# A DoRA forward kernel on Trainium2: joint runs of DRAM rows for blocks 3 and 4 and for block 6 with half of block 7, and one row stored apart

## The chip, the cores and the metric

The kernel runs on one core of one Trainium2 chip. That core has a matrix engine (TensorE, called PE in the profile, with its weight loads as PEld), a vector engine (DVE), a scalar engine (ACT), a general engine (POOL) and a synchronising engine (SP), an on-chip memory of 128 partitions (SBUF), a smaller one for matrix results (PSUM), and 16 DMA engines that move data between SBUF and DRAM. Times are device microseconds of one execution. Before the change the median of 7 runs is 163.18 us, the lowest 162.53 and the highest 163.72.

## The reference

```
W_adapted    = W + scale * (lora_A @ lora_B)
W_norm       = sqrt(sum(W_adapted ** 2, axis=0) + 1e-8)
W_final      = W_adapted / W_norm * m
y            = x.reshape(-1, 256) @ W_final
```

x has 16 x 2048 = 32768 rows of 256 float32 numbers, so a row is 1 KB and x is 32 MB; y has the same size. W is 256 x 256, the rank of lora_A and lora_B is 16. Every row of y depends on the same row of x alone, so rows may be handled in any order, as long as a result goes back to the place that its row came from.

## The kernel before

**Blocks, chunks, buffers.** The 32768 rows form 8 blocks of 4096. A block fills one buffer in SBUF, with 32 rows in each of the 128 partitions, and there are 5 buffers (`XBUFS`); block b uses buffer b mod 5. A block is 8 chunks (`CH`), a chunk 4 rows in each partition (`J`). Chunks are numbered 0 to 63 through all blocks. Results are written over the x rows that they were made from, in the same buffer, and stored from there.

**Rows in DRAM.** Which rows of x a partition gets is set by `units` (L101, L102). A unit is a stretch of consecutive rows in DRAM that is dealt out to the 128 partitions in equal consecutive runs. Before, each of the blocks 0 to 6 is one unit, so a partition's run is 32 rows, 32 KB, and the runs of neighbouring partitions begin 32 KB apart. Block 7 is two units of 16 rows each. `transfer` (L137) finds the unit of a transfer's first chunk and moves the wanted part of each partition's run, for loads and stores alike.

**Loads.** `loads` (L111 to L114) lists first chunk, count of chunks and rows in one DMA. Blocks 1, 2 and 3 come in one DMA of 4 MB each, block 4 as 24 rows and twice 4 rows, blocks 5 to 7 in halves. SP issues all of them in order; blocks 5, 6 and 7, and the last 8 rows of block 4, wait for the stores that free their buffers or that are to go first.

**Stores.** `stores` (L116 to L122) lists first chunk, count, rows in one DMA, and the chunk after which ACT issues it. The entries before `FIRST` are blocks 0 to 2. Then come, of block 3, four DMAs of 4 rows after chunk 27 and one after chunk 28; the remaining 12 rows of block 3 and all of block 4 as two DMAs after chunk 44; block 5 after chunk 47, block 6 after chunk 55, and the halves of block 7 after chunks 59 and 63. ACT drains its own writes before it issues (L282).

**The work on a chunk.** POOL rounds x to bfloat16 in pairs of chunks (L208), PE turns it (L321), DVE copies the turned block out of PSUM (L248), PE multiplies with the final weights (L335), and ACT copies the product over x in SBUF (L276). A short prologue makes the weights.

**The end.** The stores from `FIRST` on have semaphores of their own, and SP waits for each of them in turn and clears it (L360). `pieces` says how far a semaphore counts: 16 for every DMA of an entry.

Of the kernel before, what the change touches and what calls it, by code (L numbers as in the profile page):

```python
# [11 lines left out]
def kernel(  # L12
# [11 lines left out]
    P = 128  # L24
    FP32 = mybir.dt.float32
# [6 lines left out]
    N, IN = x_flat.shape  # L32
# [3 lines left out]
    J = 4  # L36
    DJ = 32
    BLK = DJ * P
    NBLK = N // BLK
# [3 lines left out]
    XBUFS = 5  # L43
    CH = DJ // J
    NCH = NBLK * CH
# [16 lines left out]
    def sb(name, shape, dtype):  # L62
        return ctx.enter_context(nc.sbuf_tensor(name, shape, dtype))
# [1 line left out]
    def ps(name, shape, dtype):  # L65
        return ctx.enter_context(nc.psum_tensor(name, shape, dtype))

    x_bufs = [sb(f"x_sb{k}", [P, DJ, IN], FP32) for k in range(XBUFS)]
    xb_bufs = [sb(f"xb{k}", [P, 2 * J, IN], BF16) for k in range(NXB)]
    xt_bufs = [sb(f"xt{k}", [P, F8, KC], BF16) for k in range(NXT)]  # L70
    w_nat = sb("w_nat", [P, KC, OUT], FP32)
# [26 lines left out]

    units = [(b * CH, CH) for b in range(NBLK - 1)]  # L101
    units += [(NCH - CH, CH // 2), (NCH - CH // 2, CH // 2)]  # L102

# [2 lines left out]
    F = NBLK - XBUFS  # L108
    G = F * CH
# [6 lines left out]
    stores = [(b * CH, CH, CH * J, 19 + b) for b in range(F - 1)]  # L116
    stores += [(G - CH, 3, 3 * J, G), (G - 5, 5, 5 * J, G)]
    FIRST = len(stores)
    stores += [(G, 4, J, G + 3), (G + 4, 1, J, G + 4)]
    stores += [(G + 5, CH - 5, (CH - 5) * J, 44), (G + CH, CH, CH * J, 44)]  # L120
    stores += [(b * CH, CH, CH * J, (b + 1) * CH - 1) for b in range(F + 2, NBLK - 1)]
    stores += [(g0, cnt, cnt * J, g0 + cnt - 1) for g0, cnt in units[-2:]]  # L122

    def pieces(entry):

        return 16 * (entry[1] * J // entry[2])


    late = [nc.alloc_semaphore(f"store{n}") for n in range(FIRST, len(stores))]
    sems = {f"store{FIRST + k}": s for k, s in enumerate(late)}  # L130

    def sem(name):
        if name not in sems:
            sems[name] = tc.alloc_semaphore(name)
        return sems[name]

    def transfer(engine, name, entry, dram, store):  # L137
        g0, cnt, rows = entry[:3]
        b, c = divmod(g0, CH)
        (u0, ucnt), = [u for u in units if u[0] <= g0 < u[0] + u[1]]  # L140
        unit = dram[u0 * J * P : (u0 + ucnt) * J * P].rearrange("(p j) k -> p j k", p=P)
        for r in range(0, cnt * J, rows):
            here = x_bufs[b % XBUFS][:, c * J + r : c * J + r + rows, :]
            there = unit[:, (g0 - u0) * J + r : (g0 - u0) * J + r + rows, :]
            src, dst = (here, there) if store else (there, here)
            engine.dma_start(out=dst, in_=src).then_inc(sem(name), 16)

    def load_x(n):
        transfer(nc.sync, f"load{n}", loads[n], x_flat, False)

    def store_y(n):
        transfer(nc.scalar, f"store{n}", stores[n], out_flat, True)

    def wait_load(engine, g):
        engine.wait_ge(sem(f"load{load_of[g]}"), pieces(loads[load_of[g]]))

    def wait_store(engine, n):
        engine.wait_ge(sem(f"store{n}"), pieces(stores[n]))
# [3 lines left out]
        out=w_nat[:], in_=W.rearrange("(p t) o -> p t o", t=KC)  # L162
    ).then_inc(sem("load_w"), 16)
    nc.scalar.dma_start(
        out=a_nat[:], in_=lora_A.rearrange("(p t) r -> p t r", t=KC)
# [3 lines left out]
    for n in range(len(loads)):  # L169
# [14 lines left out]
        out=identity[:],  # L184
        in_=zeros[:],
# [7 lines left out]
    for p in range(1, NPR):  # L193
        b, c = divmod(p, PRB)
# [9 lines left out]
        if p == REST:  # L204
            wait_store(nc.gpsimd, FIRST - 2)
        if p >= NXB:
            nc.gpsimd.wait_ge(sem("turned"), p - NXB + 1)
        nc.gpsimd.tensor_copy(  # L208
            out=xb_bufs[p % NXB][:],
            in_=x_bufs[b % XBUFS][:, 2 * c * J : 2 * (c + 1) * J, :],  # L210
# [15 lines left out]
        out=wa[:], in0=ab_ps, scalar=float(scale), in1=w_nat[:], op0=ALU.mult, op1=ALU.add  # L226
# [19 lines left out]
    for p in range(NPR):  # L246
        nc.vector.wait_ge(sem("turned"), p + 1)
        nc.vector.tensor_copy(  # L248
            out=xt_bufs[p % NXT][:].rearrange("p r t -> p (r t)").bitcast(FP32),
            in_=xt_ps[p % 2][:],  # L250
# [4 lines left out]
    for engine, idle in ((nc.gpsimd, 8), (nc.vector, 24)):  # L255
# [13 lines left out]
        out=norm[:], in_=n2_ps, func=AF.Sqrt, bias=eps_col[:]  # L269
    ).then_inc(sem("act"), 1)  # L270
    drains = 0
    for g in range(NCH):
        b, c = divmod(g, CH)
# [3 lines left out]
            out=x_bufs[b % XBUFS][:, c * J : (c + 1) * J, :], in_=y_ps[g % 2][:]  # L277
# [80 lines left out]
    for k, s in enumerate(late):  # L358
        nc.sync.wait_ge(s, pieces(stores[FIRST + k]))
        nc.sync.sem_clear(s)  # L360
# [35 lines left out]
```

## Time and profile before

| what | value |
|---|---|
| median of 7 runs | 163.18 us |
| the profiled execution | 163.25 us, span 161.9 us |
| PE busy | 94.8 us (59%) |
| ACT, POOL, DVE busy | 66.1, 60.7, 44.9 us |
| moved over DMA | 67.43 MB in 4645 packets, mean 416 GB/s |
| HBM read, written | 33.85 MB, 33.55 MB |
| last store issued by ACT | 131.46 us |

The span runs from the first to the last instruction that the profiler recorded; the execution's own time is 1.35 us more. The 40 slices of the page are each about 4 us long, a digit is a busy share in tenths. A DMA packet is one contiguous piece that one DMA engine moves. The trace also holds each packet's start, time and size, though not its engine, and the moment at which each DMA engine reports its share of a transfer as landed.

### The profile page before, as it was taken

To read this page: it belongs to the slowest core of one execution; us is meant where nothing else is said; L and a number is where in the kernel's file an instruction comes from. 1 tells how busy PE (TensorE), PEld (TensorE's weight loads), DVE (VectorE), ACT (ScalarE), POOL (GpSimd) and SP (SyncE) were. 2 spreads that over 40 slices of the span, in tenths; PEclk is the share of its full clock that TensorE was granted. 3 is DMA by queue.
4 is the path that set the end of the run, shared out by engine and by line. 5 is a ranking of instruction groups with operands and counts; after the bars stand their busy time and mean duration, and the time that the engine had idled before them with its cause. 6 is when DMAs were issued, how large, how long until landed. Compare 5 with 4: busy or idle time off the path is not lost. (4 is left out here: it accounts for less than half of the span.)

```text
span 161.9 us, 2027 instructions
## 1 busy us (share of the span) xinstructions
PE 94.8 (59%) x786; PEld 83.8 (52%) x786; DVE 44.9 (28%) x44; ACT 66.1 (41%) x68; POOL 60.7 (37%) x38
## 2 busy tenths in 40 slices
PE   0594986999999600000699999989988910000000
PEld 0282866999989400000689999979977900000000
DVE  0567233354444300000124535344533300000000
ACT  3320582767777610000047686677684640000000
POOL 1045319677672000001947675864839000000000
PEclk9998799999999985555579999999999995555555
DMA  4999999999999999999999999999999999999994
GB/s 158 431 443 465 405 478 413 413 469 413 421 388 364 494 405 397 429 413 460 405 430 423 437 424 427 443 420 415 444 492 400 413 480 407 405 486 405 397 441 206
DMA packets 4645, 67.43 MB, mean 416 GB/s; under 512 B 657, under 2 KB 674, under 8 KB 1698
## 3 DMA queue, kind: packets, MB, share of 16 engines
q1 hardware_dynamic: 2304, 33.82, 49.5%
q10 hardware_dynamic: 2338, 33.59, 48.6%
q14 instruction: 3, 0.02, 0.0%
HBM read 33.85 MB, written 33.55 MB: 416 GB/s over the span
## 5 line engine op out<-in xcount | busy, mean ns | idle before, releaser
L276 ACT COPY x_sb<-y_ps 128x1024 f32<-128x1024 f32 x64 | 62.2, 1015 | 58.7 <-PE y_ps L335 55.6
L208 POOL CAST xb<-x_sb 128x2048 bf16<-128x2048 f32 x31 | 58.2, 1893 | 64.0 <-DMA x_sb<-in_x_dram 29.3
L335 PE MATMUL y_ps<-w_final,xt 128*128 128x256 bf16 x512 | 64.7, 281 | 3.9 <-PEq L311 3.8
L248 DVE COPY xt<-xt_ps 128x1024 f32<-128x1024 f32 x32 | 39.1, 1224 | 75.0 <-PE xt_ps L321 74.9
L335 PEld LDWEIGHTS y_ps<-w_final,xt 128*128 128x128 bf16 x512 | 51.4, 101 | 11.7 <-issue 4.9
L321 PE MATMUL xt_ps<-identity,xb 128*128 128x128 f32 x264 | 35.9, 282 | 25.8 <-PEq L311 25.8
L321 PEld LDWEIGHTS xt_ps<-identity,xb 128*128 128x128 f32 x264 | 31.5, 147 | 27.2 <-issue 26.7
L264 ACT CAST xb<-x_sb 128x2048 bf16<-128x2048 f32 x1 | 1.9, 1899 | 2.7 <-DMA x_sb<-in_x_dram 2.7
L292 PE MATMUL y_ps<-identity,a_nat 128*16 128x128 f32 x2 | 0.6, 394 | 4.0 <-DMA a_nat<-in_lora_A_dram 4.0
L305 PE MATMUL y_ps<-sq,ones 128*128 128x256 f32 x4 | 2.1, 674 | 0.7 <-DVE sq L229 0.7
L262 ACT ACT_TABLE_LOAD x1 | 1.3, 1283 | 2.4 <-issue 2.4
L292 PEld LDWEIGHTS y_ps<-identity,a_nat 128*16 128x16 f32 x2 | 0.1, 90 | 4.0 <-issue 4.0
L238 DVE RECIPROCAL rnorm<-norm 128x256 f32<-128x256 f32 x1 | 1.8, 1753 | 1.5 <-ACT norm L268 1.5
L305 PEld LDWEIGHTS y_ps<-sq,ones 128*128 128x128 f32 x4 | 1.2, 323 | 1.6 <-DVE sq L229 1.5
L214 POOL MEMSET xb<- 128x2048 bf16 x1 | 1.8, 1804 | 0.0
L220 DVE CAST b_bf<-b_nat 16x256 bf16<-16x256 f32 x1 | 0.3, 281 | 3.8 <-DMA b_nat<-in_lora_B_dram 3.8
L296 PE MATMUL y_ps<-b_bf,aT 16*128 16x256 bf16 x2 | 0.6, 402 | 1.0 <-DVE aT L222 1.0
L268 ACT ACTIVATE norm<-y_ps,eps_col 128x256 f32<-128x256 f32 x1 | 0.5, 474 | 1.5 <-PE y_ps L305 1.5
L301 PE MATMUL y_ps<-m_row,ones 1*128 1x256 f32 x2 | 1.1, 630 | 0.0
L296 PEld LDWEIGHTS y_ps<-b_bf,aT 16*128 16x128 bf16 x2 | 0.1, 104 | 1.5 <-DVE aT L222 1.5
L225 DVE SCALAR_TENSOR_TENSOR wa<-y_ps,w_nat 128x512 f32<-128x512 f32 x1 | 0.7, 692 | 0.8 <-PE y_ps L296 0.8
L235 DVE TENSOR_TENSOR wam<-wa,m_all 128x256 f32<-128x256 f32 x2 | 0.8, 421 | 0.0
(14 smaller groups left out, 4.1 us busy)
## 6 DMA issues: line engine op xcount, KB each, us to landing
out_dram<-x_sb ACTq DMA_DIRECT2D x5, 4096.0 KB, 27.7
x_sb<-in_x_dram SPq DMA_DIRECT2D x7, 2048.0 KB, 29.4
x_sb<-in_x_dram SPq DMA_DIRECT2D x3, 4096.0 KB, 30.1
out_dram<-x_sb ACTq DMA_DIRECT2D x2, 2048.0 KB, 30.6
x_sb<-in_x_dram SPq DMA_DIRECT2D x1, 3072.0 KB, 47.7
out_dram<-x_sb ACTq DMA_DIRECT2D x2, 1536.0 KB, 20.7
out_dram<-x_sb ACTq DMA_DIRECT2D x1, 2560.0 KB, 32.9
out_dram<-x_sb ACTq DMA_DIRECT2D x5, 512.0 KB, 40.7
```

The source lines that it names most:

```text
L208: nc.gpsimd.tensor_copy(out=xb_bufs[p % NXB][:], in_=x_bufs[b % XBUFS][:, 2 * c * J : 2 * (c + 1) * J, :],).then_inc(sem("rounded"), 1)
L214: nc.gpsimd.memset(xb_bufs[NPR % NXB][:], 0.0).then_inc(sem("rounded"), 1)
L235: i = nc.vector.tensor_mul(out=wam[:, t], in0=wa[:, t], in1=m_all[:])
L238: nc.vector.reciprocal(out=rnorm[:], in_=norm[:]).then_inc(dv, 1)
L248: nc.vector.tensor_copy(out=xt_bufs[p % NXT][:].rearrange("p r t -> p (r t)").bitcast(FP32), in_=xt_ps[p % 2][:],).then_inc(sem("copied"), 1)
L262: nc.scalar.activation(out=warm[:], in_=eps_col[:], func=AF.Sqrt)
L264: nc.scalar.copy(out=xb_bufs[0][:], in_=x_bufs[0][:, 0 : 2 * J, :]).then_inc(sem("early"), 1)
L276: nc.scalar.copy(out=x_bufs[b % XBUFS][:, c * J : (c + 1) * J, :], in_=y_ps[g % 2][:]).then_inc(sem("room"), 1)
L301: nc.tensor.matmul(mb_ps, ones[0:1, :], m_row[:], start=True, stop=True).then_inc(pe, 1)
L305: i = nc.tensor.matmul(n2_ps, ones[:], sq[:, t, :], start=(t == 0), stop=(t == KC - 1))
L321: i = nc.tensor.transpose(xt_ps[p % 2][:, j * P : (j + 1) * P], xb_bufs[p % NXB][:, j, :].bitcast(FP32), identity[:],)
L335: i = nc.tensor.matmul(y_ps[h][:, j, :], xt_bufs[p % NXT][:, r : r + P, t], w_final[:, t, :], start=(t == 0 and (j % (J // 2)) == 0), stop ...
```

## The change

The units change. Blocks 3 and 4 become one unit of 64 rows in each partition, block 6 and the first half of block 7 one of 48 rows. Blocks 0, 1, 2 and 5 and the second half of block 7 stay as they were. So that a transfer can reach over two buffers, the five buffers become slices of one tensor `x_sb`.

The stores follow. The last 12 rows of block 3 and the 32 rows of block 4 become one entry of 44 rows, after chunk 44 as before. Block 6 and half of block 7 become one of 48 rows after chunk 59; block 6 was stored after chunk 55 before.

The entry of 44 rows, `stores[ODD]`, is issued as three DMAs: 43 rows of all 128 partitions, then the last row of the partitions 0 to 124, then the last row of the other three. They are the row "by 125 and 3 partitions on five DMA engines" of the change's description. `pieces` counts 48 for the entry. The late stores are six entries instead of eight.

The loads keep their list; those of blocks 3, 4, 6 and 7 read at other places in DRAM, by the new units.

```
-    x_bufs = [sb(f"x_sb{k}", [P, DJ, IN], FP32) for k in range(XBUFS)]
+    x_sb = sb("x_sb", [P, XBUFS * DJ, IN], FP32)
+    x_bufs = [x_sb[:, k * DJ : (k + 1) * DJ, :] for k in range(XBUFS)]
...
-    units = [(b * CH, CH) for b in range(NBLK - 1)]
-    units += [(NCH - CH, CH // 2), (NCH - CH // 2, CH // 2)]
+    units = [(b * CH, CH) for b in range(3)]
+    units += [(3 * CH, 2 * CH), (5 * CH, CH), (6 * CH, CH + CH // 2)]
+    units += [(NCH - CH // 2, CH // 2)]
...
     FIRST = len(stores)
+    ODD = FIRST + 2
     stores += [(G, 4, J, G + 3), (G + 4, 1, J, G + 4)]
-    stores += [(G + 5, CH - 5, (CH - 5) * J, 44), (G + CH, CH, CH * J, 44)]
-    stores += [(b * CH, CH, CH * J, (b + 1) * CH - 1) for b in range(F + 2, NBLK - 1)]
-    stores += [(g0, cnt, cnt * J, g0 + cnt - 1) for g0, cnt in units[-2:]]
+    stores += [(G + 5, 2 * CH - 5, (2 * CH - 5) * J, 44)]
+    stores += [(g0, cnt, cnt * J, g0 + cnt - 1) for g0, cnt in units[-3:]]
 
     def pieces(entry):
+        if entry is stores[ODD]:
+            return 16 * 3
         return 16 * (entry[1] * J // entry[2])
...
         for r in range(0, cnt * J, rows):
-            here = x_bufs[b % XBUFS][:, c * J + r : c * J + r + rows, :]
+            q = (b % XBUFS) * DJ + c * J + r
+            here = x_sb[:, q : q + rows, :]
             there = unit[:, (g0 - u0) * J + r : (g0 - u0) * J + r + rows, :]
             src, dst = (here, there) if store else (there, here)
-            engine.dma_start(out=dst, in_=src).then_inc(sem(name), 16)
+            parts = [(0, P, 0, rows)]
+            if (g0, cnt, rows) == stores[ODD][:3]:
+                parts = [(0, P, 0, rows - 1), (0, 125, rows - 1, 1), (125, 3, rows - 1, 1)]
+            for p0, n, r0, k in parts:
+                engine.dma_start(
+                    out=dst[p0 : p0 + n, r0 : r0 + k, :],
+                    in_=src[p0 : p0 + n, r0 : r0 + k, :],
+                ).then_inc(sem(name), 16)
```

## The prediction

> **What bounds the kernel now.** I read the page's slices first, then its DMA queues, then the windows over the end of the span, and last the waits of SP.
>
> The slices of the page:
>
> ```profile
> span 161.9 us, 2027 instructions
> PE   0594986999999600000699999989988910000000
> DMA  4999999999999999999999999999999999999994
> GB/s 158 431 443 465 405 478 413 413 469 413 421 388 364 494 405 397 429 413 460 405 430 423 437 424 427 443 420 415 444 492 400 413 480 407 405 486 405 397 441 206
> ```
>
> The DMA row shows nine tenths or more in 38 of the 40 slices, while PE has nothing to do after the 33rd slice. No compute engine sets the end: the sixteen DMA engines do, and they run out of work only in the last slice. A change counts only if it alters the work of the DMA engine that finishes last, or leaves that engine without work.
>
> The queues and the issues of the page, loads on q1 and stores on q10:
>
> ```profile
> q1 hardware_dynamic: 2304, 33.82, 49.5%
> q10 hardware_dynamic: 2338, 33.59, 48.6%
> q14 instruction: 3, 0.02, 0.0%
> out_dram<-x_sb ACTq DMA_DIRECT2D x5, 4096.0 KB, 27.7
> out_dram<-x_sb ACTq DMA_DIRECT2D x5, 512.0 KB, 40.7
> ```
>
> A 4 MB store lands 27.7 us after its issue though its own bytes take about 9.7 us (below): stores wait in a long queue, so the moment at which ACT issues one matters little.
>
> Windows of the end; the last columns are clock, DMA share and GB/s, put down to the packets that start in the window:
>
> ```profile
> 120.00:135.00 15.00, 8.84 (x80) 7.74 (x77) 2.75 (x3) 7.66 (x8) 5.48 (x3) 0.97 1.03 444
> 135.00:150.00 15.00, 0.00 (x0) 0.00 (x0) 0.00 (x0) 0.00 (x0) 0.00 (x0) 0.50 0.99 425
> 158.00:160.00 2.00, 0.00 (x0) 0.00 (x0) 0.00 (x0) 0.00 (x0) 0.00 (x0) 0.50 0.94 401
> 160.00:161.90 1.90, 0.00 (x0) 0.00 (x0) 0.00 (x0) 0.00 (x0) 0.00 (x0) 0.50 0.04 17
> ```
>
> In the last 1.90 us 17 GB/s start, which is 32 KB: two packets of 16 KB. One engine works on while fifteen have finished. The trace's landing records say the same: of the last store's sixteen landings thirteen lie between 160.07 and 160.61 us (median 160.32), two at 160.88 and 160.90, the last at 161.90. That one engine sets the end. Its packet records tell why: ten 32 KB packets in a row between 122.0 and 134.8 us took 1236 to 1325 ns, where 1213 is usual, 0.68 us too long in sum. The 160.9 pair are engines that also fetched instructions (the q14 packets).
>
> SP's waits, which end the program:
>
> ```profile
> SPq L360 <- DMA out_dram<-x_sb: 28.2, 4, 9.7
> ```
>
> SP waits for each late store in turn, 9.7 us for one of 4 MB, and ends with the last landing.
>
> **Prices of a packet.** By the packet records one partition's run is one packet: 4 KB 159 ns, 16 KB 611, 32 KB 1213, and the next packet of the engine starts 4 ns before the end. So a KB costs (1213 - 159)/28 = 37.6 ns and a packet 159 - 150.6 - 4 = 4.4 ns besides; the closing mark of a transfer, 4 bytes, costs 9 - 4 = 5 ns.
>
> **The change part by part.**
>
> *Joint stores.* Each joint transfer takes 8 packets and one mark from every engine: 8 x 4.4 + 5 = 40 ns, for two of them -0.08 us on all sixteen.
>
> *Joint runs in DRAM.* The rows of blocks 3 and 4 now lie 64 KB apart from partition to partition (32 before), those of blocks 6 and 7a 48 KB. All loads keep their count and packet sizes. No run shows another pitch. The nearest rows: packets of one size take the same time in every block (32 KB, 1213 ns), so I take 0. For a bound, the last two load packets of block 4 on all engines (47.5 to 50.7 us) took together some 1.2 us more than their usual 912 ns each, for no cause that I can name: -1.2 if the new pitch ends that, +1.2 if it brings a second such stall.
>
> The Trainium skill bears on this, "DMA: Bandwidth & Descriptors", section "Latency and other measured facts": large power-of-two row pitches in HBM slow copies, 207 GB/s at 512 KiB against 214 at full rate and 103 at 4 MiB. No run here shows it. Applied as it stands, an estimate for 64 KB is under 3% of the 16.8 MB that these two blocks move, under 1.3 us; by it the sum would be up to 165.1, by the row 163.8.
>
> *The odd row.* All sixteen engines lose one 1 KB row in each of 8 partitions: 8 x 37.6 = -0.30 us. Five engines get 25 packets of 1 KB each, and three of these one more. What does such a packet cost? The line above gives 4.4 + 37.6 = 42 ns; the steady 2 KB packets of w_nat (84 ns) agree. But the only 1 KB packets of the trace, 17 of b_nat and m_row, took 44 to 46 ns thirteen times and 153, 338, 352 and 366 ns four times: mean 106, so 0.10 us each. I keep 0.042 and 0.10 as ends and take 0.10: it is the row of the same size, and b_nat too is one partition's KB by engines that serve other partitions otherwise; here other engines read the same partitions' neighbourhood at full rate meanwhile. Five engines then change by -0.08 - 0.30 + 25 x 0.10 = +2.12, three of them +2.22; the other eleven by -0.38.
>
> The skill's same page, section "Why a DMA increments its semaphore by 16 and not by 1", states that the engine count is the largest number up to 16 that divides the partitions: 125 gives 5, 3 gives 3, on the lowest-numbered engines. The trace agrees as far as it goes: m_row, one partition, has a single landing of data where others have sixteen. Its section "Rules for kernel authors" advises a multiple of 16 partitions outermost, so that all engines share the work, which speaks against this row; spread that way the estimate would be 163.1.
>
> *ACT's queue.* After chunk 44 three issues stand in place of two, each 0.34 to 0.91 us (L146's shortest and longest), so at most 0.9 us more before ACT's copy of chunk 45; PE behind it waits for its PSUM buffer. All loads are issued by 86.4 us, so nothing upstream suffers. The last store goes out at 131.5 us and its predecessor's data start to be the queue's head only near 152: some 20 us of cover. Block 6's store goes out with 7a's at 126.2 instead of 119.4 us; the store ahead of it lands until 142.5, so 14 us of cover remain. If that cover were gone the whole 6.8 us delay would show. Here: 0. An issue and a drain fall away after chunk 55; hidden likewise.
>
> *SP's queue.* Six waits instead of eight at the end, clears of 25 to 35 ns; all but the last lie before the last landing: 0. POOL, DVE and PE keep their instructions.
>
> **The sum.** A typical engine's last landing, 160.32, becomes 160.32 + 2.22 = 162.54 on the five; the late engine, if one of the eleven, 161.90 - 0.38 = 161.52. The end moves from 161.90 to 162.54: +0.64. The profiled execution took 163.25, 1.35 beyond its span, so 163.89; it stands 0.07 above the median of 163.18, which becomes 163.82.
>
> **The rivals.**
>
> *Slower in another way: the late engine is one of the five.* Even at 42 ns it gets -0.38 + 26 x 0.042 = +0.71: 163.9. At 0.10 us it would be +2.2: 165.4. Five of sixteen speak for it; the records carry no engine numbers.
>
> *Nearly the same: small packets at the line's price, late engine among the eleven.* Five engines end at 160.32 + 0.71 = 161.03, the late one at 161.52: -0.38, 162.8. Up to a price of (161.90 + 0.38 - 160.32)/26 = 0.075 us a packet there is no loss. For it speak thirteen of the seventeen 1 KB packets. Against it: an instruction-fetching engine among the five ends at 161.6.
>
> *Faster: the late engine's slow packets go.* They lie in the store of block 4 and the next one. If its 32 KB runs at a pitch of 32 KB caused them, the joint runs take away 0.68 as well: 161.90 - 0.38 - 0.68 = 160.84, and the five at 161.03 to 161.2 set the end, -0.75: 162.4. It decides if 0.2 us of the 0.68 goes and the small packets stay under about 0.06 us. Against it: the slowness followed one engine, not the transfer.
>
> *It doesn't do what it says.* If 125 partitions spread over sixteen engines, eight packets each, only -0.08 stays: 163.1, the same.
>
> **How the numbers follow.** About 0.3% (0.49 us) is what a measurement of this kernel can tell from no change. Slower by more than that: 0.50, of which 0.28 by costly small packets, 0.18 by the late engine among the five, 0.04 by pitch. Same: 0.22, of which 0.18 small packets at the line's price and 0.04 no such spreading. Faster: 0.28, by the late engine's slow packets or the 1.2 us stall gone. The likeliest gives 163.8, its own range 163.6 to 164.6. The range for all runs from 162.4, the faster rival, to 165.0; beyond lie some 0.08 at each end (both slower causes together, or the stall gone as well).
>
> **What would show it.** Right: the page counts some 4490 packets for 4645 (256 large ones and 24 marks less, 128 of 1 KB more); the 1 KB packets take 100 ns in the mean; the last store's landings part into eleven early and five late ones. Wrong: 1 KB packets at 46 ns; the last landing again a single one; slow loads in blocks 3 and 4.

## The result and the profile after

The changed kernel takes 163.60 us (median of 21 runs, 163.12 to 163.89); the kernel before 163.04 us (54 runs, the first seven among them). The ratio is 1.0034, with a 95% interval from 1.0025 to 1.0044: slower by 0.34%, some 0.56 us. The forecast was slower, 163.8 us, and the range 162.4 to 165.0 holds the time. The reason that carried most of the forecast was wrong all the same, so it hit the time by luck; a rival had the reason.

The page of the changed kernel, first the slices and the packets, then the issues of stores:

```profile
span 161.9 us, 2024 instructions
DMA  5999999999999999989999999999999899998994
GB/s 166 426 445 461 413 486 397 413 486 397 421 419 455 413 478 410 437 367 453 385 423 422 408 457 426 403 445 438 409 466 499 381 383 502 488 415 389 401 397 182
DMA packets 4493, 67.43 MB, mean 417 GB/s; under 512 B 633, under 2 KB 778, under 8 KB 1802
out_dram<-x_sb ACTq DMA_DIRECT2D x1, 6144.0 KB, 23.3
out_dram<-x_sb ACTq DMA_DIRECT2D x1, 5504.0 KB
```

The DMA engines are busy from start to end as before. The packets are 4493, where 4645 were counted before: 256 large ones and 24 marks less, 128 of 1 KB more. The transfer of 43 rows (5504 KB) and that of 48 rows (6144 KB) went out as single transfers.

Windows over the end of the changed kernel, with the columns as before (clock, DMA share and GB/s last):

```profile
158.00:159.00 1.00, 0.00 (x0) 0.00 (x0) 0.00 (x0) 0.00 (x0) 0.00 (x0) 0.50 0.80 344
159.00:160.00 1.00, 0.00 (x0) 0.00 (x0) 0.00 (x0) 0.00 (x0) 0.00 (x0) 0.50 0.35 147
160.00:161.90 1.90, 0.00 (x0) 0.00 (x0) 0.00 (x0) 0.00 (x0) 0.00 (x0) 0.50 0.10 43
```

After 160 us 43 GB/s x 1.90 us = 82 KB still start, five packets of 16 KB, where it was two before. The landings of the last store say how many engines that is: ten between 159.34 and 159.56 us, then 160.66, 160.83, 161.11, 161.16, 161.47 and 161.85. Before, thirteen lay within 0.54 us, two followed at 160.9 and one came in late alone.

SP's waits and ACT's issues at the end, from the waits and the timeline of the changed kernel:

```profile
SPq L375 <- DMA out_dram<-x_sb: 20.3, 3, 14.5
```

```profile
103.75 1.13 ACTq L158 DMA_DIRECT2D out_dram<-x_sb  x3
108.27 0.36 ACTq L158 DMA_DIRECT2D out_dram<-x_sb  x1
133.74 0.36 ACTq L158 DMA_DIRECT2D out_dram<-x_sb  x1
139.41 0.34 ACTq L158 DMA_DIRECT2D out_dram<-x_sb  x1
```

The 48-row store went out at 133.74 us, not at the 126.2 that I had read off the kernel before, and the last one at 139.41 instead of 131.46. The last load landed at 125.1 instead of 120.1 us: in the packet records an engine takes its loads and its stores in turn, packet by packet. Between two 16 KB load packets of 611 ns each there lay a store packet of 12 KB, 460 ns, toward the end of the loads before (117 us), and there lies one of 43 KB, 1627 ns, now. So the loads get a smaller share. This cost nothing, because the store ahead in the queue landed from 140.0 us on; of the 14 us of cover that I had counted, about 6 were left.

**Why the two spans are alike.** Both profiled executions have a span of 161.9 us (163.25 us before, 163.20 us after, the latter not among the 21 runs), though the medians are 0.56 us apart. The packet records show a part of what sets single executions apart. Between 47 and 51.5 us, where loads end and stores begin, large packets of the kernel before took 0.88 us an engine too long (slices 12 and 13 of its page, 388 and 364 GB/s, against 419 and 455 here). In the changed kernel that sum is 0.01 there and 0.46 between 77 and 84.5 us. Over the eleven profiles of this text the first stall is there in three (0.88, 0.69, 0.86 us) and nearly absent in eight (under 0.1). It comes with the old units and with the new, so it is no work of the change. One pair of profiles can't show a difference of half a microsecond here; the median can, and so can the landings' order at the end.

### The profile page after: what moved, and what is told of

It is laid out like the page before. It is cut to its first block, busy times and chain, and to the rows that moved or that the text cites. A ratio compares the mean times of both kernels' runs of the same rounds, so it can differ in the third digit from the quotient of the medians.

```text
span 161.9 us, 2024 instructions
## 1 busy us (share of the span) xinstructions
PE 99.8 (62%) x786; PEld 87.4 (54%) x786; DVE 44.9 (28%) x44; ACT 66.1 (41%) x68; POOL 60.9 (38%) x38
## 2 busy tenths in 40 slices
DMA packets 4493, 67.43 MB, mean 417 GB/s; under 512 B 633, under 2 KB 778, under 8 KB 1802
## 5 line engine op out<-in xcount | busy, mean ns | idle before, releaser
L350 PE MATMUL y_ps<-w_final,xt 128*128 128x256 bf16 x512 | 66.4, 286 | 4.6 <-PEq L326 4.6
L350 PEld LDWEIGHTS y_ps<-w_final,xt 128*128 128x128 bf16 x512 | 52.3, 103 | 13.3 <-issue 5.7
L336 PE MATMUL xt_ps<-identity,xb 128*128 128x128 f32 x264 | 38.9, 297 | 28.4 <-PEq L326 28.4
L336 PEld LDWEIGHTS xt_ps<-identity,xb 128*128 128x128 f32 x264 | 34.1, 155 | 29.9 <-issue 29.3
L316 PEld LDWEIGHTS y_ps<-m_row,ones 1*128 1x128 f32 x2 | 0.5, 308 | 0.5 <-DMA m_row<-in_m_dram 0.5
```

Of the source, the lines that this page charges most:

```text
L316: nc.tensor.matmul(mb_ps, ones[0:1, :], m_row[:], start=True, stop=True).then_inc(pe, 1)
L336: i = nc.tensor.transpose(xt_ps[p % 2][:, j * P : (j + 1) * P], xb_bufs[p % NXB][:, j, :].bitcast(FP32), identity[:],)
L350: i = nc.tensor.matmul(y_ps[h][:, j, :], xt_bufs[p % NXT][:, r : r + P, t], w_final[:, t, :], start=(t == 0 and (j % (J // 2)) == 0), stop ...
```

## The experiments

Each ratio is against runs of the kernel before that were taken beside that experiment, with its 95% interval; it is not the quotient of the two medians. The code shown leaves out the lines of `pieces`, which count the DMAs of the entry.

**The joint runs alone.** The 44 rows in one transfer by 128 partitions:

```
-            if (g0, cnt, rows) == stores[ODD][:3]:
-                parts = [(0, P, 0, rows - 1), (0, 125, rows - 1, 1), (125, 3, rows - 1, 1)]
```

> The changed kernel without the odd row: the 44 rows go in one transfer by 128 partitions. Theory A (the row on five engines costs, the joint runs are free): in the profile of the changed kernel the five engines end 1.3 to 2.2 us after the ten early ones; without the row they lose 25 packets of 42 ns and all get 0.30 us back, so -0.7 us against the changed kernel: 0.9990 of the kernel before (0.998 to 1.000). Rival B (the new pitch of rows or the long packets cost): still 1.003 of the kernel before. Rival C (both cost a part): 1.001 to 1.002.

Measured: 0.9998, interval 0.9979 to 1.0017; median 162.74 us. The end of its span, in windows:

```profile
159.00:160.00 1.00, 0.00 (x0) 0.00 (x0) 0.00 (x0) 0.00 (x0) 0.00 (x0) 0.50 0.24 98
160.00:161.40 1.40, 0.00 (x0) 0.00 (x0) 0.00 (x0) 0.00 (x0) 0.00 (x0) 0.50 0.03 12
```

12 GB/s x 1.40 us is one packet of 16 KB: one engine alone at the end again (last landings 159.97, 160.70, 160.94, 161.40). The joint runs neither cost nor gain anything that can be measured. That rules out the pitch of 64 KB and the long packets as the cause of the 0.34%.

**The odd row alone.** The kernel before with its own units and stores, but the last row of block 4 apart:

```
+    ODD = (G + CH, CH, CH * J)
...
+            if store and (g0, cnt, rows) == ODD:
+                parts = [(0, P, 0, rows - 1), (0, 125, rows - 1, 1), (125, 3, rows - 1, 1)]
```

> The kernel before, with its own runs and stores, but the last row of block 4 stored apart by 125 and 3 partitions. Theory A, with the late engine among the five: +0.72 us, 1.0044 of before (1.003 to 1.006). Rival B (pitch or long packets cost, the row is harmless): 0.998 to 1.000. Rival D (the late engine is not among the five and a 1 KB packet costs 42 ns): 0.998 to 0.999.

Measured: 1.0046, 1.0026 to 1.0065. The medians, 163.38 us against 163.01, are closer, 1.0022, the means 1.0036, from eight runs of this kernel. With the joint runs at no cost, the whole loss comes with the row. The end of its span:

```profile
159.00:160.00 1.00, 0.00 (x0) 0.00 (x0) 0.00 (x0) 0.00 (x0) 0.00 (x0) 0.50 0.31 131
160.00:161.80 1.80, 0.00 (x0) 0.00 (x0) 0.00 (x0) 0.00 (x0) 0.00 (x0) 0.50 0.09 36
```

36 GB/s x 1.80 us are four packets of 16 KB: several engines work on while the others have finished, as in the changed kernel.

**Two rows.** The changed kernel with twice the dose:

```
-                parts = [(0, P, 0, rows - 1), (0, 125, rows - 1, 1), (125, 3, rows - 1, 1)]
+                parts = [(0, P, 0, rows - 2)]
+                for r1 in (rows - 2, rows - 1):
+                    parts += [(0, 125, r1, 1), (125, 3, r1, 1)]
```

> The changed kernel with two rows by 125 and 3 partitions instead of one. Theory A: the last engines are among the five already, so each further row costs its full 25 x 42 - 301 ns = +0.75 us: 1.0034 + 0.0046 = 1.008 of before (1.006 to 1.010). Rival B: 1.002 to 1.004, as for one row. If a 1 KB packet delayed its engine by 100 ns (the recorded prediction): +2.2 us, 1.017.

Measured: 1.0099, 1.0074 to 1.0125. The windows:

```profile
159.00:160.00 1.00, 0.00 (x0) 0.00 (x0) 0.00 (x0) 0.00 (x0) 0.00 (x0) 0.50 0.35 147
160.00:163.30 3.30, 0.00 (x0) 0.00 (x0) 0.00 (x0) 0.00 (x0) 0.00 (x0) 0.50 0.15 65
```

The second row costs at least as much as the first: the ten early engines end where they did (159.39 to 159.76 us), one lands at 160.38, five from 161.65 to 163.25. Most of its 256 packets of 1 KB took 46 ns, the longest 55, and the next of an engine starts 41 to 43 ns after the one before. So each packet holds its engine for some 42 ns, and 100 ns, with an expectation of 1.017, is out.

**The same row on all sixteen engines.** The changed kernel with `(0, P, rows - 1, 1)` as the second part and no third:

```
-                parts = [(0, P, 0, rows - 1), (0, 125, rows - 1, 1), (125, 3, rows - 1, 1)]
+                parts = [(0, P, 0, rows - 1), (0, P, rows - 1, 1)]
```

> The changed kernel with the odd row stored apart as well, but by all 128 partitions, so over all sixteen engines. Theory A (what costs is that five engines get the whole row): like the joint runs alone plus 8 packets and a mark, +0.04 us: 0.9992 of before (0.998 to 1.000). Rival E (a row of 1 KB packets or one more transfer is costly wherever it goes): 1.003 or more.

Measured: 0.9985, 0.9966 to 1.0004. The end of its span has one packet of 16 KB again (13 GB/s x 1.30 us):

```profile
159.00:160.00 1.00, 0.00 (x0) 0.00 (x0) 0.00 (x0) 0.00 (x0) 0.00 (x0) 0.50 0.16 66
160.00:161.30 1.30, 0.00 (x0) 0.00 (x0) 0.00 (x0) 0.00 (x0) 0.00 (x0) 0.50 0.03 13
```

Packets of 1 KB and one more transfer are harmless here; what costs is that five engines get the whole row. To tell 0.9985 from no change I ran it again:

> Once more the changed kernel with the odd row stored by all 128 partitions, to tell 0.9985 from no change. By the packet prices it is the joint runs plus 0.04 us, so 0.999 to 1.0005; below 0.9985 again would mean that the joint runs gain more than 0.08 us.

Measured: 0.9990, 0.9972 to 1.0008. Both lie a little under 1, and neither can be told from it.

**Which engine is late.** The packet records have no engine numbers. But a load on one to five partitions puts one packet on each of as many engines, as the counts below show, and a packet of a size of its own can be found again. Six small loads into a scratch tile, put into the kernel before (shown) and, behind the store of 44 rows, into the joint runs:

```
+                if stores[n][:2] == (G + 5, CH - 5):
+                    for i, k in enumerate((1, 2, 3, 4, 5, 16)):
+                        w = 40 + 8 * i
+                        nc.scalar.dma_start(
+                            out=scratch[0:k, 80 * i : 80 * i + w], in_=x_flat[0:k, 0:w]
+                        ).then_inc(sem(f"probe{i}"), 16)
```

> The kernel before, with six tiny loads into a scratch tile put behind the 12-row store of block 3: 1, 2, 3, 4, 5 and 16 partitions, each with packets of a size of its own (160 to 320 bytes), so that their packets name the engines in the packet records. They add at most 0.1 us to an engine. Theory A (the late engine of the kernel before is one of the five that the odd row uses): the engine with the row of slow 32 KB packets carries at least one of the sizes of the loads on 1 to 5 partitions, and so do the engines that fetch instructions. Rival D: it carries the 16-partition size alone, as 11 of 16 engines do.

> The joint runs without the odd row, with the same six tiny loads behind the store of 44 rows. Theory A: the slow engine and the two or three engines that fetch instructions carry sizes of the loads on 1 to 5 partitions, the same ones as in the kernel before. If the slow engine changes from run to run by chance, it carries another set of sizes than there.

Measured, from the packet records (start in ns, size in bytes, duration in ns), around the slow engine. Consecutive packets of an engine overlap by 3 to 5 ns, which is how they are chained:

```
kernel before with probes                  joint runs with probes
120640, 120751, 120938, 120946:            130860, 130897, 130973, 131402:
   the four packets of 256                    the four packets of 256
121645   288   19                          131755   288   26
121688 32768 1287   (usual: 1213)          131806 32768 1338   (usual: 1213)
122972 32768 1293                          133140 32768 1293
124261 32768 1293                          134429 32768 1265
```

In both kernels the fifth 288-byte packet, late and by itself, runs directly ahead of the slow 32 KB packets, and no 256-byte packet is near. The sizes are nested: one engine carries all six, the next all but that of one partition, and so on. So the engine that carries the load on five partitions but not the one on four is called the fifth here, and it is the slow engine in both. The engines that fetched instructions at 128.1 and 131.9 us carried the sizes of 3, 4 and 5 and of 4 and 5 partitions in the kernel before: the third and the fourth. In the joint runs the fetches at 137.0 and 137.1 us fell on the fourth and the third. (Chains of equal packets that end within a few ns of each other can be swapped; for the slow engine the packets stand next to each other, for the fetches the chain goes over some ten packets.)

That these engines are among the five that 125 partitions use can be seen in the changed kernel without probes. A lane is the chain of packets of one engine: of the five lanes with packets of 1 KB one has the slow 32 KB packets (133.0 to 142.0 us) and ends last, and two have the instruction fetches at 139.8 and 144.6 us. The slow lane has 25 packets of 1 KB, none of the last three. With the odd row alone and with two rows, too, the lane that ends last has both packets of 1 KB and slow large ones. The sixth late landing of the changed kernel, 160.66 or 160.83 us, belongs to a lane without 1 KB packets; it was some 1.2 us behind at 131.3 us already, and what made it late I don't know.

**Sparing the five.** If the late engines are the first five, work should go to the others. ACT's transfers on fewer partitions used the first engines each time, as the probes show, so I tried POOL's queue, in two ways. First three rows of block 4, 121 partitions by POOL and 7 by ACT:

```
+                parts = [(0, P, 0, rows - 3), (121, 7, rows - 3, 3)]
+                if engine is nc.gpsimd:
+                    parts = [(0, 121, rows - 3, 3)]
...
+    nc.gpsimd.dma_start(out=scratch[0:5, :], in_=x_flat[0:5, 0:64]).then_inc(sem("turn"), 16)
+    nc.gpsimd.wait_ge(sem("done"), 6)
+    transfer(nc.gpsimd, "apart", stores[FIRST + 2], out_flat, True)
```

> The joint runs, with the last three rows of block 4 taken out of the large store: 121 partitions go by a transfer that POOL issues at its end, after a small load on 5 partitions, the other 7 by ACT. If POOL's transfers take turns over the engines (5 and then 11 of them), the five engines lose 24 packets' KB, 0.90 us, and get at most one packet of 3 KB back, the other eleven get 11 packets of 117 ns, +0.4 us: the late ones end some 0.7 us earlier and the others at about the same time, 0.994 to 0.997 of the kernel before. If they spread over all sixteen, eight partitions each, the gain is gone: 0.999 to 1.001. If POOL's issue is slow or its packets stall the others: above 1.002.

Measured: 1.0001, 0.9986 to 1.0015. POOL's transfer did not take turns: it made 60 packets of 6 KB and one of 3 KB, four on nearly every engine, the slow one included. (Waiting for it, POOL held up PE's last step, and the last store went out at 150.1 us; the store ahead landed from 154.6, so that too was hidden.) Then 16 partitions, 112 to 127, over 20 rows, in 11 and 5, the other 112 by ACT:

```
+    R = 20
...
+                parts = [(0, P, 0, rows - R), (0, 112, rows - R, R)]
+                if engine is nc.gpsimd:
+                    parts = [(112, 11, rows - R, R)] if name == "apart0" else [(123, 5, rows - R, R)]
```

> The joint runs, with the last 20 of the 44 rows stored by 112 partitions from ACT (7 on each engine) and the remaining 16 partitions by POOL in 11 and 5, each behind a small load on 5 partitions. If POOL's transfers of up to 16 partitions take one engine for a partition and go on where the last one stopped, no large share falls to the first five engines: they lose 20 x 37.6 ns = 0.75 us each, five others gain as much, six stay. The late engine would then end 0.75 us earlier: 0.995 to 0.997 of the kernel before. If POOL's transfers always begin at the first engine, the first five carry two partitions instead of one: +0.75 us, 1.004 or more.

Measured: 1.0153, 1.0110 to 1.0196, from the three shortest of six runs; the six spread from 164.98 to 168.48 us. Its stores by POOL as the DMA view has them (size and us to landing):

```profile
out_dram<-x_sb POOLq DMA_DIRECT2D x1, 220.0 KB, 14.9
out_dram<-x_sb POOLq DMA_DIRECT2D x1, 100.0 KB, 19.1
```

220 KB took until 14.9 us after the issue. By the packet records POOL's sixteen 20 KB packets took from 761 ns, the usual time, up to 3994 ns, eleven of them over 2.2 us; eight of them began within 0.7 us of each other. That they held each other up because many engines read neighbouring partitions at once is a guess that no run tests. This says nothing for or against sparing the five; the attempt brought a cost of its own that is larger. A version that clearly beats the kernel before was not found.

## Why the prediction was right or wrong

**What bounds the kernel.** Right. PE, ACT and POOL stayed idle at the end in every run, and the differences, but for the last attempt with POOL, whose cause is open, followed from the work of single DMA engines. The reading that one engine alone sets the end was right too.

**Joint stores, -0.08 us, and the pitch, 0 in -1.2 to +1.2.** Right within what can be told: together 0.9998. The stall that I used as a bound comes and goes by execution with either pitch, and 1.2 us was too large for it: by the packet records it was 0.58 to 1.16 us on the sixteen engines, 0.88 in the mean. The page's rule on large row pitches in the Trainium skill ("DMA: Bandwidth & Descriptors", section "Latency and other measured facts") begins at 512 KiB; at 64 KB no run here shows such a loss.

**The odd row's shares.** The five engines with 25 packets each, and one more on three of them, are as stated: the rule of that page's section "Why a DMA increments its semaphore by 16 and not by 1", 5 engines for 125 partitions and 3 for 3, fits the trace, which has lanes with 25 and with 26 packets of 1 KB. The last landings parted into ten early and six late ones, where eleven and five were forecast.

**The price of a 1 KB packet, 0.10 us.** This is the step that failed. It was also the sign of being wrong that the prediction named. The 128 packets took 46 ns each, one of them 53, so 42 ns with the overlap: the price that the line through 4 and 32 KB packets gave, and thirteen of the seventeen 1 KB packets. I took the mean over the seventeen, though its four large values, 153 to 366 ns, came between 3.5 and 4.0 us of the span, within about two microseconds of the first load packet (1.9 us). At 42 ns a typical engine among the five ends at 160.32 + 0.71 = 161.03, before the late one; by this alone the change would have cost nothing.

**The late engine among the eleven.** This step failed too. The sum put the engine there without saying why (161.90 - 0.38 = 161.52). It is the fifth of the five. With the right price that gives the rival's sum, with 25 packets in place of the rival's 26, since the slow lane has none of the last three: 161.90 - 0.38 + 25 x 0.042 = 162.57, +0.67 us or 0.41%. Measured were 0.34% (0.25 to 0.44) for the change and 0.46% (0.26 to 0.65) for the row alone, where the sum is -0.30 + 25 x 0.042 = +0.75 us, 0.46%. I gave this rival 0.18, for five engines of sixteen; the slow lane and the lanes with instruction fetches were visible in the same packet records, but not which engines they were.

So the mark, slower by some 0.6 us, came by luck out of two errors that cancelled: a packet price too high by a factor of 2.4, and a late engine on the wrong side.

**ACT's and SP's queues, 0.** Right in the price, wrong in the working for the 48-row store: 133.74 instead of 126.2 us, as told above. I had moved the issue by the chunk numbers and not asked what longer store packets do to the loads that run beside them.

**The faster rival.** It fell: the slow 32 KB packets stayed with the joint runs, on the same engine.

## What to carry to other kernels

When DMA engines set the end, count work per engine, not per queue: a transfer that uses fewer engines only helps if the engine that finishes last is not among them, and in the runs where the lanes could be told the last one, and those with the late instruction fetches, were among the five that this transfer used. Price a small packet from steady packets, not from a mean that holds start-up. Before comparing two single profiles, look at how far single runs of one kernel spread and at which stalls come and go.

## What I had not expected

The fifth DMA engine had a row of slow 32 KB packets, most of them 1227 to 1338 ns instead of 1213, from about 122 us on in one and from 132 us on in the other of the two kernels that I probed, and one engine with such packets was there in every profile; what else uses that engine at that time was not tried.

Longer store packets slowed the loads beside them: with packets of 41 to 44 KB the last load landed at 123.6 to 125.1 us in the kernels with joint runs, with 24 and 20 KB at 121.9, with 12 KB at 119.7 to 120.2.

Packets of 20 KB that POOL's queue stored from 16 neighbouring partitions took up to 3994 ns instead of 761; why is open. The 1 KB packets of the odd row, at most 55 ns, showed nothing of the kind.
